# A hybrid decoder block on one core: the mixer's side work put in another order

## The chip, the core and the metric

The kernel runs on one core of a Trainium2 chip. The core has five engines with queues of their own: TensorE (PE, matmuls; the loads of its stationary operand are shown apart as PEld), VectorE (DVE), ScalarE (ACT), GpSimd (POOL) and SyncE (SP), and 16 DMA engines. Each engine works through its own list of instructions in order and waits on semaphores for the others. The metric is the time of one launch on the device, in microseconds (us).

## What is computed

One layer of a decoder block for 512 tokens of 1024 channels, in FP32. A modulation vector gives shift, scale and gate for the two halves. The first half, the mixer, projects the normalised tokens with one large matrix and feeds two branches: four retention heads, and four heads of a gated delta rule behind a short causal convolution. The second half is a mixture of 16 experts. Cut to what the change touches:

```python
mod = silu(c) @ mod_w + mod_b                       # 6 x 1024 columns
rq, rk, rv, rg, gq, gk, gv, gz, ga, gb, gate_a, gate_b = split_columns(xm @ w_in)
# retention, per head: (rope(q) k^T * decay) v, then RMS norm of each head's 256 columns
o_r = rms_norm(retention(rope(rq), rope(rk), rv));  y_ret = silu(rg) * o_r
# delta rule
qkv = silu(causal_conv(concat(gq, gk, gv), conv_w))  # 4 taps along the tokens
q, k = l2_normalize(...), l2_normalize(...)
beta = sigmoid(gb);  log_decay = -exp(a_log) * softplus(ga + dt_bias);  g_cum = cumsum(log_decay)
o_g = rms_norm(delta_rule(q, k, v, g_cum, beta)) * silu(gz)
h = x + gate * ((sigmoid(gate_a) * y_ret + sigmoid(gate_b) * o_g) @ w_out)
h = h + gate2 * moe(rms_norm(h) * (1 + scale2) + shift2)
```

## The kernel before

**The main projection.** Its columns are cut into blocks of 256: RQ0, RQ1, RK0, RK1 (T blocks), RV0 to RV3 (N blocks), the small block G with the eight columns ga and gb, then the T blocks GQ0, GQ1, GK0, GK1, GV0 to GV3, and the N blocks RG, GTA, GZ, GTB, four of each. A T block gives channels by tokens, an N block tokens by channels. Every FP32 operand is split into a rounded part hi (ScalarE, L293) and the rest lo (DVE, L294), and each product takes three passes. A block has two halves g (a T half has 24 matmuls, an N half 48, all at L1064), and `split_w(b + 1, ...)` splits the next block's weights meanwhile.

**The side work** stands in Python generators. Behind every piece of matmuls (8 in a T block, 16 in an N block, so three pieces in a half) the loop takes one step of `mods`, one of `convs` and one of `side`: what a generator issues up to its next `yield` goes into the engines' queues there. That alone sets the order on each engine; a step is no time, and a queue that comes late holds up whatever stands behind.

- `mods` (L488 to L520): the remaining 32 columns of the modulation. GpSimd fetches 512 KB (rawm, two buffers, L493), multiplies (L391) and adds 1024 to 128 in three operations (L393); PE sums over partitions with a matmul to one column (modp, L510) and DVE adds the bias (mcol, L511). The fetch of the next round is issued behind the column. While `state["subs"]` is set no round begins. Behind the last column PE transposes all of them (L516). At the first half of GZ0 the loop steps `mods` until it is done.
- `convs`: for each T half of GQ, GK and GV the convolution (ty: one ScalarE operation at L648, three of DVE at L650), the sigmoid (sg, L653), the product (gqT, gkT or vt, L656 and L678), then for GQ and GK the squares' sums on PE (L667) and for GV a transposition (vt, L684) and a scale (gv, L689).
- `side`: `gab_gen` turns ga and gb into beta and the cumulative decay (copy of g at L608; chain of small DVE operations L614 to L628; matmul gc at L632; transposition gct at L638). `ret_gen(h)`, one head after another, computes the scores (rs, L570), multiplies them by the decay into PT (L576, one buffer), sums outputs into PSUM (ro, L563) four steps later, takes squares' sums and copies the outputs over rv (ScalarE), and then norms them: a root on DVE, `rsqrt`, of 12 operations (L171 to L179), and two scales of rv (L586). Retention is done over the whole triangle of 512 tokens. Then `triangles` prepares the delta rule's triangular matrices (pre, L710; kk, L719) and solves them on GpSimd. The delta rule's chunks (`gdn_gen`) begin when that has been stored, with a transposition (tq, L762).

All PSUM tiles of the side work come from six banks in turn, `pst(...)`; a bank is taken again when the work on it six tiles ago is done. The main projection has two banks of its own.

## Time and profile before

| | us |
|---|---|
| median of three runs | 1087.81 |
| lowest and highest | 1086.55, 1091.23 |
| the profiled execution's own time | 1090.74 |
| its span in the trace | 1088.9 |
| PE busy in the span | 963.6 (88%) |
| DVE busy | 741.9 (68%) |
| ACT busy | 518.4 (48%) |
| POOL busy | 310.3 (28%) |

The stages by time in the trace: norm, modulation and first loads up to 61; RQ and RK to 90; RV to 138; G to 144; GQ, GK and GV to 302; RG from there, with GTA, GZ and GTB to about 577; output projection and routing to about 690; the experts to about 1040 and the tail. The trace names for each wait the instruction that ended it. The granted clock of PE is given as a share of its full speed: 1.0 is 2.4 GHz and 0.5 is 1.2 GHz.

### The profile page before, as it was taken

The page shows a single profiled execution, that of the slowest core. Times are in us where ns is not written, and L with a number is a line of the kernel's source. Part 1 is how long each engine was busy: PE and PEld are TensorE (multiplying, and loading weights), DVE is VectorE, ACT ScalarE, POOL GpSimd, SP SyncE. Part 2 cuts the span into 40 slices and gives each one's busy share as a digit, 9 for nine tenths or more (in the row PEclk, how much of TensorE's full clock was granted, in tenths as well). Part 3 has the DMA queues.
Part 4 walks back from the last instruction along what each step waited for, and adds up shares of the span by engine and source line. Part 5 has one row for each costly group of instructions (what it writes and reads, how often), then busy time and mean ns, then how long its engine had stood idle before and what let it go on. Part 6 is the DMA issues. An engine that isn't in the chain of part 4 may idle for free. (4 is left out here: it accounts for less than half of the span.)

```text
span 1088.9 us, 14847 instructions
## 1 busy us (share of the span) xinstructions
PE 963.6 (88%) x5672; PEld 834.7 (77%) x5672; DVE 741.9 (68%) x1163; ACT 518.4 (48%) x750; POOL 310.3 (28%) x285
## 2 busy tenths in 40 slices
PE   4899988989889999999989966699968899999973
PEld 2579957768788999999989965478756688888752
DVE  3478245767886673465458593699766889889777
ACT  4453134433342332263233433478645888878623
POOL 2018733553447555000010154111100211111144
PEclk8999998999989999999999988799989999999895
DMA  9857742232345532322157346789684999999931
GB/s 297 264 177 249 223 138 82 86 110 84 125 138 140 169 102 93 88 88 78 43 171 258 115 143 88 270 303 388 247 313 154 333 389 381 377 378 370 338 134 77
DMA packets 139538, 217.91 MB, mean 200 GB/s; under 512 B 14942, under 2 KB 72830, under 8 KB 138692
## 3 DMA queue, kind: packets, MB, share of 16 engines
q1 hardware_dynamic: 124640, 182.45, 49.3%
q0 software_dynamic: 11296, 30.66, 9.2%
q10 hardware_dynamic: 3524, 3.78, 1.0%
q8 instruction: 47, 0.77, 0.3%
q14 instruction: 31, 0.25, 0.1%
HBM read 204.98 MB, written 21.16 MB: 208 GB/s over the span
## 5 line engine op out<-in xcount | busy, mean ns | idle before, releaser
L294 DVE TENSOR_TENSOR lo<-raw,hi 128x1024 fp32r<-128x1024 f32 (+1 forms) x194 | 242.3, 1287 | 61.6 <-ACT hi L293 61.5
L293 ACT CAST hi<-raw 128x1024 fp32r<-128x1024 f32 (+1 forms) x198 | 197.5, 1043 | 34.6 <-PE gu L1492 27.3
L1064 PE MATMUL pm<-lo,xh 128*128 128x256 f32 x640 | 185.7, 290 | 12.2 <-DVE ty L650 7.0
L1064 PE MATMUL pm<-hi,xh 128*128 128x256 f32 x640 | 185.3, 290 | 0.0
L1064 PE MATMUL pm<-hi,xl 128*128 128x256 f32 x640 | 184.9, 289 | 0.0
L1064 PEld LDWEIGHTS pm<-lo,xh 128*128 128x128 f32 x640 | 124.9, 195 | 13.1 <-issue 7.2
L1064 PEld LDWEIGHTS pm<-hi,xh 128*128 128x128 f32 x640 | 124.9, 195 | 0.5
L1064 PEld LDWEIGHTS pm<-hi,xl 128*128 128x128 f32 x640 | 124.8, 195 | 0.3
L1492 PE MATMUL gu<-lo,xth 128*128 128x512 f32 x256 | 104.8, 409 | 10.3 <-DVE lo L1559 8.7
L1492 PE MATMUL gu<-hi,xtl 128*128 128x512 f32 x256 | 103.9, 406 | 2.0 <-DVE xtl L1460 2.0
L1492 PE MATMUL gu<-hi,xth 128*128 128x512 f32 x256 | 104.2, 407 | 0.0
L393 POOL TENSOR_TENSOR rawm<-rawm 128x512 f32<-128x512 f32 (+2 forms) x96 | 101.5, 1057 | 7.7
L493 POOL DMA_DIRECT2D rawm<-in_mod_w_dram x32 | 29.6, 925 | 210.7 <-PE modp L510 199.0
L1064 PE MATMUL pm<-xl,hi 128*128 128x512 f32 x168 | 70.1, 417 | 2.0 <-ACT hi L293 1.6
L1064 PE MATMUL pm<-xh,lo 128*128 128x512 f32 x168 | 71.3, 424 | 0.5 <-DVE lo L294 0.5
L1064 PE MATMUL pm<-xh,hi 128*128 128x512 f32 x168 | 70.9, 422 | 0.0
L1492 PEld LDWEIGHTS gu<-lo,xth 128*128 128x128 f32 x256 | 50.1, 196 | 23.3 <-DVE lo L1559 9.1
L1451 POOL DMA_INDIRECT X<-xfd,toks x14 | 20.2, 1446 | 151.8 <-PE xe L1472 131.4
L1008 ACT ACTIVATE sg<-pm 128x512 f32<-128x512 f32 x32 | 18.9, 597 | 91.1 <-PE pm L1064 77.1
L1514 PE MATMUL py<-lo,th 128*128 128x512 f32 x144 | 60.1, 417 | 1.3 <-ACT th L1505 1.3
L391 POOL TENSOR_TENSOR rawm<-rawm,cs 128x1024 f32<-128x1024 f32 x32 | 61.1, 1910 | 0.6
L1492 PEld LDWEIGHTS gu<-hi,xtl 128*128 128x128 f32 x256 | 50.0, 195 | 14.7 <-DVE xtl L1460 2.4
(405 smaller groups left out, 2056.4 us busy)
## 6 DMA issues: line engine op xcount, KB each, us to landing
raw<-in_w_in_dram SPq DMA_DIRECT2D x32, 1024.0 KB, 5.8
raw<-in_w_up_dram SPq DMA_DIRECT2D x26, 1024.0 KB, 13.6
raw<-in_w_gate_dram SPq DMA_DIRECT2D x24, 1024.0 KB, 11.0
raw<-in_w_down_dram SPq DMA_DIRECT2D x20, 1024.0 KB, 14.9
rawm<-in_mod_w_dram POOLq DMA_DIRECT2D x32, 512.0 KB, 5.2
rawe<-in_w_down_dram SPq DMA_DIRECT2D x9, 1024.0 KB, 16.0
rawe<-in_w_up_dram SPq DMA_DIRECT2D x8, 1024.0 KB, 16.9
mod<-in_mod_w_dram SPq DMA_DIRECT2D x7, 1024.0 KB, 12.5
```

What stands on the lines that cost most here:

```text
L293: act.copy(out=hi, in_=rw)
L294: (eng or dve).tensor_tensor(out=lo, in0=rw, in1=hi.bitcast(F32), op=ALU.subtract)
L391: pool.tensor_tensor(out=r, in0=r, in1=cs.unsqueeze(2).to_broadcast([P, KB, n]), op=ALU.mult)
L393: pool.tensor_tensor(out=r[:, :m], in0=r[:, :m], in1=r[:, m:2 * m], op=ALU.add)
L493: pool.dma_start(out=r, in_=mw[:, :, (16 + i) * P:(17 + i) * P])
L1008: act.activation(out=sg, in_=pt, func=AF.Sigmoid)
L1064: pe.matmul(o, lhsT=l, rhs=r, start=st, stop=sp__)
L1451: pool.indirect_dma_start(out=X, out_offset=None, in_=xfd, in_offset=bass.IndirectOffsetOnAxis(ap=at, axis=0), bounds_check=S - 1, oob_is_ ...
L1492: pe.matmul(pt, lhsT=xx[a][k // 4][:, k % 4], rhs=hi_lo[w][:, k % 4], start=(k == 0 and i == 0), stop=(k == KB - 1 and i == 2))
L1514: pe.matmul(pt, lhsT=tt[a][:, k], rhs=hi_lo[w][:, k], start=(k == 0 and i == 0), stop=(k == 3 and i == 2))
```

## The change

- **Retention** becomes one generator. It makes 16 score steps (four heads by four), issues an output's sums five steps behind its scores (`RL = 5`), uses a second PT buffer for the odd heads, copies a head out when its four outputs are issued, and takes one root for all four heads and then the eight scales, one head a step.
- **The modulation sums** go into two accumulators (acc) outside the fetched tile. A column is issued one round later, behind the sum of the next round. A round comes every three steps, in GQ, GK and GV every six. `subs` is set when the triangles begin, and not when their solution begins.
- **The gate block**: the weights of GQ0 are split ahead of the copy of g; the matmul gc is issued four side steps behind the chain and not one.
- **The triangles** issue the pre operations in steps of two, not four; the chunks of the delta rule wait four steps, not two, between the loads and the transposition tq.

```diff
-    def pool_sum(r, n):
+    def pool_sum(r, n, o):
...
-        for m in (4, 2, 1):
+        for m in (4, 2):
             pool.tensor_tensor(out=r[:, :m], in0=r[:, :m], in1=r[:, m:2 * m], op=ALU.add)
-        return r[:, 0]
+        pool.tensor_tensor(out=o, in0=r[:, 0], in1=r[:, 1], op=ALU.add)
...
+        accs = [tm.tile([P, P], F32, tag=f"acc{i}", name="acc", bufs=1) for i in range(2)]
+
+        def column(i):
+            pt = pst("modp")
+            pe.matmul(pt[:, :1], lhsT=accs[i % 2], rhs=ones[:, 0:1], start=True, stop=True)
+            dve.tensor_tensor(out=mcol[:, i:i + 1], in0=pt[:, :1], in1=cols[:, 16 + i:17 + i], op=ALU.add)
+
         nxt = fetch(0)
         for i in range(4 * KB):
             r = nxt
-            yield
+            for _ in range(6 if state.get("slow") else 3):
+                yield
             while state.get("subs"):
                 yield
             if i + 1 < 4 * KB:
                 nxt = fetch(i + 1)
             next(fills, None)
-            acc = pool_sum(r, P)
-            for _ in range(3 if i else NM):
-                yield
-            pt = pst("modp")
-            pe.matmul(pt[:, :1], lhsT=acc, rhs=ones[:, 0:1], start=True, stop=True)
-            dve.tensor_tensor(out=mcol[:, i:i + 1], in0=pt[:, :1], in1=cols[:, 16 + i:17 + i], op=ALU.add)
+            pool_sum(r, P, accs[i % 2])
+            if i:
+                column(i - 1)
+        for _ in range(4):
+            yield
+        column(4 * KB - 1)
...
+        n = NT * H
+        for s_ in range(n + RL + 1):
+            mul = scores(s_ // NT, s_ % NT) if s_ < n else None
+            o = s_ - RL
+            if 0 <= o < n:
+                out(o // NT, o % NT)
+            if o > 0 and o % NT == 0:
+                for i in range(2):
+                    evac(o // NT - 1, i)
+            yield
+            if mul:
+                mul()
+        for _ in range(2):
+            yield
+        rsqrt(st[:, 16:32], st[:, 0:16], 1.0 / DV, EPS)
+        for h in range(H):
+            yield
+            for i in range(2):
+                o = rv[i][:, :, h * DV:(h + 1) * DV]
+                dve.tensor_tensor(out=o, in0=o, in1=st[:, 16 + h * 4 + 2 * i:18 + h * 4 + 2 * i].unsqueeze(2)
+                                  .to_broadcast([P, 2, DV]), op=ALU.mult)
+            done["ret", h] = True
...
-        yield
+        for _ in range(4):
+            yield
         pt = pst("gc")
...
         sub = pool
+        state["subs"] = True
...
-            yield
+                if h % 2:
+                    yield
         act.activation(out=pre[:, NT:], in_=pre[:, NT:], func=AF.Exp, scale=-1.0)
...
-        yield
-        yield
+        for _ in range(4):
+            yield
         Q = u("Q")
...
+        state["slow"] = GQ <= c0 < GQ + 8 * 256
...
+            for hf in nxt:
+                split_w(b + 1, hf)
             side.add(gab_gen(pt))
             next(side.gens[-1])
-            for hf in nxt:
-                split_w(b + 1, hf)
```

**On DVE in the GK blocks.** The queue of DVE before, at the end of the first head's root (st) and up to the split of the next weights; PT is a block of masked scores, ty the convolution, rv the retention's values and outputs:

```order
L178 SCALAR_TENSOR_TENSOR na<-na,nx 128x4
L179 SCALAR_TENSOR_TENSOR st<-na,ny 128x4
L586 TENSOR_TENSOR rv_467<-rv_467,st 128x2x256
L586 TENSOR_TENSOR rv_468<-rv_468,st 128x2x256
L511 TENSOR_TENSOR mcol<-modp,cols 128x1
L576 TENSOR_TENSOR PT<-rs,decay 128x512
L576 TENSOR_TENSOR PT<-rs,decay 128x384
L650 SCALAR_TENSOR_TENSOR ty<-pm,cols,ty 128x511
L650 SCALAR_TENSOR_TENSOR ty<-pm,cols,ty 128x510
L650 SCALAR_TENSOR_TENSOR ty<-pm,cols,ty 128x509
L656 TENSOR_TENSOR gkT<-ty,sg 128x512
L294 TENSOR_TENSOR lo_93<-raw_88,hi_92 128x1024
```

And in the changed kernel, in the GK blocks too:

```order
L294 TENSOR_TENSOR lo_93<-raw_88,hi_92 128x1024
L502 TENSOR_TENSOR mcol<-modp,cols 128x1
L576 TENSOR_TENSOR PT<-rs,decay 128x512
L294 TENSOR_TENSOR lo_93<-raw_88,hi_92 128x1024
L576 TENSOR_TENSOR PT<-rs,decay 128x384
L576 TENSOR_TENSOR PT<-rs,decay 128x256
L677 SCALAR_TENSOR_TENSOR ty<-pm,cols,ty 128x511
L677 SCALAR_TENSOR_TENSOR ty<-pm,cols,ty 128x510
L677 SCALAR_TENSOR_TENSOR ty<-pm,cols,ty 128x509
L683 TENSOR_TENSOR gkT<-ty,sg 128x512
L576 TENSOR_TENSOR PT<-rs,decay 128x128
```

The root and the scales of rv are gone from here; all four PT operations of the third head stand here, where before the second head's began, among the convolutions and the lo of the splits.

**On DVE ahead of the last GV convolutions and RG0.** Before, the last head's scales and half of pre (the preparation of the triangles; gv are scaled values of the delta rule):

```order
L179 SCALAR_TENSOR_TENSOR st<-na,ny 128x4
L586 TENSOR_TENSOR rv_467<-rv_467,st 128x2x256
L586 TENSOR_TENSOR rv_468<-rv_468,st 128x2x256
L294 TENSOR_TENSOR lo_93<-raw_88,hi_92 128x1024
L710 SCALAR_TENSOR_TENSOR pre<-pre,gcum,sq 128x128 x4
L511 TENSOR_TENSOR mcol<-modp,cols 128x1
L710 SCALAR_TENSOR_TENSOR pre<-pre,gcum,sq 128x128 x4
L689 TENSOR_TENSOR gv_852<-vt,br 128x2x128
L689 TENSOR_TENSOR gv_853<-vt,br 128x2x128
L650 SCALAR_TENSOR_TENSOR ty<-pm,cols,ty 128x511
```

After, with the scales of two heads at the same place (rst holds all heads' roots):

```order
L294 TENSOR_TENSOR lo_91<-raw_89,hi_90 128x1024
L502 TENSOR_TENSOR mcol<-modp,cols 128x1
L612 TENSOR_TENSOR rv_467<-rv_467,rst 128x2x256
L612 TENSOR_TENSOR rv_468<-rv_468,rst 128x2x256
L294 TENSOR_TENSOR lo_91<-raw_89,hi_90 128x1024
L612 TENSOR_TENSOR rv_467<-rv_467,rst 128x2x256
L612 TENSOR_TENSOR rv_468<-rv_468,rst 128x2x256
L738 SCALAR_TENSOR_TENSOR pre<-pre,gcum,sq 128x128 x2
L716 TENSOR_TENSOR gv_854<-vt,br 128x2x128
L716 TENSOR_TENSOR gv_855<-vt,br 128x2x128
L677 SCALAR_TENSOR_TENSOR ty<-pm,cols,ty 128x511
```

The root of all heads begins 22 rows ahead of these, and the scales of the first two heads right behind it; the six other pre follow behind the convolution's product.

**On GpSimd in the first rounds of the modulation.** Before, a fetch behind the second sum, which waits for PE's column since it writes the tile that the column reads:

```order
L391 TENSOR_TENSOR rawm<-rawm,cs 128x1024
L393 TENSOR_TENSOR rawm<-rawm 128x512
L393 TENSOR_TENSOR rawm<-rawm 128x256
L393 TENSOR_TENSOR rawm<-rawm 128x128
L493 DMA rawm<-in_mod_w_dram 128x8x128
L391 TENSOR_TENSOR rawm<-rawm,cs 128x1024
```

After:

```order
L391 TENSOR_TENSOR rawm<-rawm,cs 128x1024
L393 TENSOR_TENSOR rawm<-rawm 128x512
L393 TENSOR_TENSOR rawm<-rawm 128x256
L394 TENSOR_TENSOR acc<-rawm 128x128
L493 DMA rawm<-in_mod_w_dram 128x8x128
L391 TENSOR_TENSOR rawm<-rawm,cs 128x1024
```

The last sum writes acc, and the fetch that follows needs only GpSimd's own sum; PE's columns are what a round waits for only from the third sum's acc onwards.

## Rows read from the trace of the kernel before

**Rows 1.** The page: busy time of the engines, then GB/s in 40 slices.

```profile
PE 963.6 (88%) x5672; PEld 834.7 (77%) x5672; DVE 741.9 (68%) x1163; ACT 518.4 (48%) x750; POOL 310.3 (28%) x285
...
GB/s 297 264 177 249 223 138 82 86 110 84 125 138 140 169 102 93 88 88 78 43 171 258 115 143 88 270 303 388 247 313 154 333 389 381 377 378 370 338 134 77
```

**Rows 2.** Waits of PE, 60 to 600: who waited for whom: total, times, longest us.

```profile
PE ro L563 <- DVE PT L576: 7.2, 3, 4.9
PE pm L1064 <- DVE ty L650: 7.0, 1, 7.0
PE pm L1064 <- ACT sg L1008: 5.1, 2, 2.9
PE gc L632 <- DVE glog L628: 4.0, 1, 4.0
PE modp L510 <- POOL rawm L393: 2.8, 2, 2.5
PE tq L762 <- DMA T<-dt: 2.0, 1, 2.0
PE pm L1064 <- ACT hi L293: 1.6, 1, 1.6
```

**Rows 3.** Windows: stretch, length, PE, PEld, DVE, ACT, POOL busy, granted clock, DMA share, GB/s.

```profile
145.49:253.70 108.21, 96.50 (x422) 77.84 (x423) 72.55 (x125) 40.23 (x69) 47.25 (x40) 0.91 0.34 105
253.70:302.23 48.53, 41.57 (x203) 34.30 (x201) 41.09 (x81) 17.35 (x36) 23.32 (x22) 0.95 0.42 130
147.66:151.07 3.41, 3.41 (x9) 2.08 (x8) 2.60 (x4) 0.62 (x1) 1.60 (x2) 0.50 0.55 163
164.72:174.96 10.24, 8.79 (x27) 7.44 (x28) 6.20 (x14) 5.93 (x8) 0.87 (x2) 0.50 0.00 0
239.82:246.65 6.83, 5.01 (x12) 3.97 (x13) 5.68 (x10) 0.96 (x2) 3.39 (x4) 0.50 0.60 192
297.84:308.08 10.24, 5.77 (x27) 5.80 (x28) 7.71 (x23) 4.25 (x4) 1.48 (x2) 0.50 0.33 103
352.45:355.86 3.41, 3.41 (x18) 3.41 (x18) 3.19 (x3) 0.00 (x0) 2.86 (x3) 0.50 0.94 225
362.69:366.10 3.41, 3.41 (x19) 3.41 (x18) 0.92 (x1) 1.68 (x2) 0.00 (x0) 0.50 0.05 17
```

**Rows 4.** Timeline of ACT at the gate block's end: start, duration, engine, line.

```profile
143.92 0.57 ACT L608 COPY g<-pm 8x512 f32<-8x512 f32 x1 [4.96 <-PE pm L1045]
```

**Rows 5.** Timelines of DVE and POOL in GQ0, the gate chain.

```profile
160.23 2.75 DVE L618 SCALAR_TENSOR_TENSOR tz<-tz 128x16 f32<-128x16 f32 x1
...
161.03 1.91 POOL L391 TENSOR_TENSOR rawm<-rawm,cs 128x1024 f32<-128x1024 f32 x1
```

**Rows 6.** Timelines of DVE and PE, first head's root, scales, PT, outputs.

```profile
203.40 1.25 DVE L171 TENSOR_SCALAR nx<-st 128x4 f32<-128x4 f32 x1
...
207.49 1.29 DVE L586 TENSOR_TENSOR rv<-rv,st 128x512 f32<-128x512 f32 x2
...
208.77 1.14 DVE L576 TENSOR_TENSOR PT<-rs,decay 128x512 f32<-128x512 f32 x2
...
209.50 0.70 PE L563 MATMUL ro<-rv,PT 128*128 128x256 f32 x2 [1.88 <-DVE PT L576]
```

**Rows 7.** Groups of instructions on PE, 145.4 to 302.2: count, busy, mean, idle.

```profile
L563 PE MATMUL ro<-rv,PT 128*128 128x256 f32 x80 | 21.5, 398 | 7.2 <-DVE PT L576 7.2
```

**Rows 8.** Timeline of DVE ahead of RG0: four pre, three convolution operations.

```profile
297.03 1.13 DVE L710 SCALAR_TENSOR_TENSOR pre<-pre,gcum,sq 128x128 f32<-128x128 f32 x4
...
299.87 2.30 DVE L650 SCALAR_TENSOR_TENSOR ty<-pm,cols,ty 128x511 f32<-128x511 f32 x3
```

**Rows 9.** Timeline of POOL: the second fetch's wait, a round's three adds.

```profile
77.31 0.93 POOL L493 DMA_DIRECT2D rawm<-in_mod_w_dram  x1 [56.26 <-PE modp L510]
...
95.60 4.71 POOL L393 TENSOR_TENSOR rawm<-rawm 128x512 f32<-128x512 f32 x3
```

**Rows 10.** Windows: RV, 90 to 138, columns as in rows 3.

```profile
90.00:138.00 48.00, 47.78 (x396) 47.30 (x395) 19.43 (x19) 11.28 (x17) 38.06 (x32) 1.00 0.74 225
```

More of the change, by code (lines that the diff above doesn't have):

```diff
@@ L551, in rope, with ret_gen, scores, out @@
         dve.tensor_tensor(out=rqk[:, h2], in0=rqk[:, h2], in1=sw, op=ALU.add)
-    def ret_gen(h):
-        PT = rp.tile([P, 1280], F32, tag="PT", name="PT", bufs=1)
+    def ret_gen():
+        RL = 5
         offs = [0, 512, 896, 1152]
-        po = []
-        def out(i):
+        PTs, pos_ = {}, {}
+        st = small.tile([P, 32], F32, name="rst")
+        def scores(h, jb):
+            if jb == 0:
+                PTs[h] = (slot(2, [P, 1280], F32, "PT") if h % 2 else
+                          rp.tile([P, 1280], F32, tag="PT", name="PT", bufs=1))
+            n = S - jb * P
+            pt = pst("rs")
+            pe.matmul(pt[:, :n], lhsT=rqk[:, H + h, jb * P:(jb + 1) * P], rhs=rqk[:, h, jb * P:],
+                      start=True, stop=True)
+            return lambda: dve.tensor_tensor(out=PTs[h][:, offs[jb]:offs[jb] + n], in0=pt[:, :n],
+                                             in1=decay[:, h, :n], op=ALU.mult)
+        def out(h, i):
@@ L559, in out @@
             if i % 2 == 0:
-                po.append(pst("ro"))
+                pos_.setdefault(h, []).append(pst("ro"))
             for jb in range(i + 1):
                 a = offs[jb] + (i - jb) * P
-                pe.matmul(po[-1][:, (i % 2) * DV:(i % 2 + 1) * DV], lhsT=PT[:, a:a + P],
+                pe.matmul(pos_[h][-1][:, (i % 2) * DV:(i % 2 + 1) * DV], lhsT=PTs[h][:, a:a + P],
                           rhs=rv[jb // 2][:, jb % 2, h * DV:(h + 1) * DV], start=(jb == 0), stop=(jb == i))
-        for jb in range(NT + 4):
-            if jb < NT:
-                n = S - jb * P
-                pt = pst("rs")
-                pe.matmul(pt[:, :n], lhsT=rqk[:, H + h, jb * P:(jb + 1) * P], rhs=rqk[:, h, jb * P:],
-                          start=True, stop=True)
-            if jb >= 4:
-                out(jb - 4)
-            yield
-            if jb < NT:
-                dve.tensor_tensor(out=PT[:, offs[jb]:offs[jb] + n], in0=pt[:, :n], in1=decay[:, h, :n], op=ALU.mult)
@@ L577, in ret_gen @@
-        st = tm.tile([P, 8], F32, tag="st", name="st", bufs=3)
-        for i in range(NT):
-            sumsq(po[i // 2][:, (i % 2) * DV:(i % 2 + 1) * DV], st[:, i:i + 1])
-        for i in range(2):
-            act.copy(out=rv[i][:, :, h * DV:(h + 1) * DV], in_=po[i].rearrange("p (t q) -> p t q", t=2))
-        yield
-        rsqrt(st[:, 4:8], st[:, 0:4], 1.0 / DV, EPS)
-        for i in range(2):
-            o = rv[i][:, :, h * DV:(h + 1) * DV]
-            dve.tensor_tensor(out=o, in0=o, in1=st[:, 4 + 2 * i:6 + 2 * i].unsqueeze(2).to_broadcast([P, 2, DV]),
-                              op=ALU.mult)
@@ L588, in ret_gen, with evac @@
-        done["ret", h] = True
+        def evac(h, i):
+            po = pos_[h][i]
+            for j in range(2):
+                sumsq(po[:, j * DV:(j + 1) * DV], st[:, h * 4 + i * 2 + j:h * 4 + i * 2 + j + 1])
+            act.copy(out=rv[i][:, :, h * DV:(h + 1) * DV], in_=po.rearrange("p (t q) -> p t q", t=2))
+        n = NT * H
[7 more added lines that the diff above has]
+                    evac(o // NT - 1, i)
+            yield
+            if mul:
+                mul()
@@ L733, in triangles @@
                 yield
-                state["subs"] = True
             to = [P, LB - 1 - c, c + 1]
@@ L756, in gdn_gen @@
         sp.dma_start(out=h4(pr), in_=gcd[ch * H:(ch + 1) * H].unsqueeze(0).to_broadcast([P, H, P]))
-        yield
-        yield
+        for _ in range(4):
+            yield
         Q = u("Q")
@@ L1131, in rets @@
             def rets():
-                for h in range(H):
-                    yield from ret_gen(h)
+                yield from ret_gen()
                 yield from triangles()
```

## The prediction

> **What bounds the kernel now.** I read the page first: TensorE (PE) is busy for 963.6 of 1088.9 us [rows 1]. It is the bound, so a change to the side work can only take back time in which PE stands still or runs at half clock. Next the waits of PE in the mixer, by the instruction that ended them, from 60 to 600 us [rows 2]. Six of the seven rows name work that the change touches: the retention's outputs wait 7.2 us for the masked scores PT on VectorE (DVE), the main projection 7.0 us for a convolution (ty) on DVE, the cumulative decay (gc) 4.0 us for glog, the modulation column (modp) 2.8 us for GpSimd's sum, the transposition tq 2.0 us for a DMA, and the first GQ block 1.6 us for a rounded weight (hi). The row of sg, 5.1 us, belongs to the end of the mixer and stays. Last, the granted clock by stretches [rows 3]: behind each of these waits stands a stretch at 0.5, the lower level (1.2 GHz). Half of PE's busy time in such a stretch is lost: 3.41 / 2 = 1.7 us at 147.66, 8.79 / 2 = 4.4 at 164.72, 5.01 / 2 = 2.5 at 239.82, 5.77 / 2 = 2.9 at 297.84, 1.7 at 352.45 and 1.7 at 362.69, so 14.9 in all. Every one begins at or behind a wait of at least 1.6 us. I take it that it goes with the wait. Behind the mixer PE is again the bound, and nothing there depends on when the mixer ends, so a gain in the mixer reaches the end.
>
> **The change part by part.** Terms are in us against the profiled execution's own 1090.74 (span 1088.9 and 1.8 around it), which lies 2.9 above the median of the runs, 1087.81.
>
> 1. *Splits of GQ0 ahead of the gate block's side work.* ScalarE's copy of g stood idle for 4.96 until 143.92, for the block's last matmul, and takes 0.57 [rows 4]; the rounding of the next block's weights stood behind it. Now it stands ahead, in that idle time. The wait of 1.6 and its half-clock stretch go; the 0.5 behind the second half's lo too. 1.6 + 0.5 + 1.7: **-3.8** (between -2.1 and -3.8).
>
> 2. *gc four side steps later.* The chain to glog ran on DVE from about 160 to 166. One of its 16-column operations took 2.75 there, beside GpSimd's multiplication that began at 161.03 and took 1.91 [rows 5]. PE waited 4.0 for the end and then lost 4.4. Four steps are 32 matmuls of the projection, at 96.50 / 422 = 0.23 [rows 3] some 7 us, which is more than the 4.0. I leave 1 for the places behind it (gct, and the l2 scales that use its result): -4.0 - 4.4 + 1 = **-7.4** (between -4 and -8.4).
>
> 3. *One root chain in place of four.* For each head 12 tiny DVE operations ran from 203.40 to 207.49 and two rv scales of 1.29 behind them; only then came the next head's PT, at 208.77, and PE waited 1.88 for it [rows 6]. In the new order PT has no root ahead of it. The 7.2 and the 2.5 of half clock go: **-9.7** (between -5 and -9.7).
>
> 4. *Retention is denser, and this is my largest unknown.* All four heads now end in GV0, two blocks earlier. About one head's outputs move into the stretch before 253.70: 21.5 / 4 = 5.4 of PE time [rows 7], **+5.4** there, and the same off the stretch behind it (in term 5). With side work this dense, PE is tied to DVE through six PSUM banks: a score's bank comes free only when its PT is through, and PT stands in DVE's queue behind a convolution (2.30 for three, [rows 8]) and one or two lo. I laid the DVE durations against PE's steps half-block by half-block over the ten half-blocks GQ0 to GV0, and got waits of about 9, most of them in GK1 and GV0; with 3 for clock, **+12**. Lower bound 0: DVE is busy 72.55 of 108.21 there [rows 3], loses two roots, and two steps of PE might cover its backlog. Upper bound 24: ten half-blocks at 1.9 (the wait before one PT) with half a us or so of clock each. I take the middle, since the new order has the backlog of convolution and lo but not that of the root.
>
> 5. *GV1 to RG0.* The root (once), the rv scales of all heads (eight operations) and eight more pre operations land here. Before, this took 48.53 us with DVE busy for 41.09 [rows 3], and a backlog that let PE wait 7.0. DVE's sum after: 41.1, less two roots (8.2) and a head's PT (about 2), plus one root (4.1), two more pairs of scales (2.6) and eight pre (2.3 by the row of four, 1.13 [rows 8]) = 39.9. Of DVE's 7.4 idle before I keep 3. That gives 43, bound by DVE: -5.5, and the half clock that reached past 302 gives half a us more, **-6** (0, if DVE's idle time stays as it is and the pre operations cost double, to -9).
>
> 6. *GpSimd.* Sums now go to two accumulators and PE reads a column one round later; the rounds pause while GpSimd solves the triangles. The wait of 2.5 near 352 and its 1.7, and the wait of tq for its DMA near 362 (the loads now stand two yields further ahead of it) with its 1.7, go: **-7.9** (between -4 and -7.9). Three columns are left for a drain at GZ0, where PE meets them back to back: **+2.5**, from 0 (sums ready) to 6 (one round, below).
>
> 7. *The start.* GpSimd stood idle for 56.26 up to 77.31, since its next fetch waited for PE's column [rows 9]. Without that wait two more fetches of 0.5 MB fall into the first 50 us, where the DMA moves 297 and 264 GB/s in the first two slices [rows 1], twice the 105 and 130 of the mixer's middle [rows 3], and the first loads are what all else waits for: 1 MB / 0.3 MB per us = **+3** (0 to 6, the upper end if GpSimd's two sums also hold up DVE).
>
> 8. *The longer drain of chunks 2 and 3 at GTB*, bound by PE: **+0.5** (0 to 2).
>
> Sum: -3.8 - 7.4 - 9.7 + 5.4 + 12 - 6 - 7.9 + 2.5 + 3 + 0.5 = -11.4, so 1079.3 in a profile and 1087.8 - 11.4 = **1076.4** as a median.
>
> The row of 2.75 for 16 columns shows DVE standing still until GpSimd's multiplication ends. The Trainium skill ("SBUF — State Buffer", Who interferes with whom) says that a DVE instruction with two SBUF inputs and a GpSimd instruction that reads SBUF exclude one another for a whole instruction, and the trace agrees: the operation ends at 162.98, the multiplication at 162.94. By that rule the twelve rounds between 145 and 302 that become seven free DVE of some five multiplications, at most 10 us, which would make the sum about -15; by the rows, which show PE waiting for DVE at a few places only, it is nothing that I can count, and I leave it out.
>
> **The rivals.** *The clean case:* the backlog of term 4 is covered, no wait comes and the clock stays up. Then -11.4 - 12 = -23.4, 1064.4, or 1066 with a us or two left over. For it: DVE has a third of its time free before 253.70. Against it: that is a mean, and the waits in [rows 2] come from bursts. *Coupling:* term 4 at its upper end, 24 in place of 12: 1088.4, nothing gained. For it: one root alone made PE wait 1.88, a convolution and two lo are as long, and the clock falls behind waits of 1.6 already. *The change does not reach its place:* its two safest edits (terms 1 and 2, -11.2) depend on nothing else, so this would be about what coupling gives, and shares its chance. *The slow case, GpSimd bound in RV:* from 90 to 138 GpSimd was busy for 38.06 with 32 instructions, five to a round: 5.9 a round [rows 10]. The new order has eight columns there in place of six, one per three side steps, about 6 us. At 5.9 and with one round of lead this just holds. But a round beside much DVE work took 0.93 + 1.91 + 4.71 = 7.5 [rows 5, 9]; eight of these are 60 in 48, less a lead of about one round, 7.5: PE waits some 4.5 in RV, and each wait may cost a half-clock stretch of 1.7 to 4.4. With four of these at 3 that is 16.5, and the rounds that are late come back at the drain (6 in place of 2.5): -11.4 + 16.5 + 3.5 = +8.6, **1096**. It decides from 17 us of new waits in RV and at the drain upwards; a wait of PE for acc in RV of more than a us would be its mark. Against it: the mean of 5.9, in which such long rounds are already counted.
>
> **How the numbers follow.** My forecast, the middle of term 4: 0.47. Clean: 0.18. Coupling: 0.23. GpSimd bound: 0.12. The forecast and the clean case are both faster by over 0.5% (below 1082.4), which is about what a measurement of this kernel can tell from no change; the coupling is within it, the last slower (above 1093.2). So 0.65, 0.23, 0.12. The range leaves out the slow case and the lower half of the clean one: 1066 to 1092, where the upper end is coupling with the start at its 6.
>
> **What the profile after would show.** Right: no wait of gc for glog nor of ro for PT above a us, a first GQ block without gap, clock 1.0 from 145 to 175; GV0's convolution done about 5 earlier and RG0 about 11 earlier. PE's new waits, for banks (rs, ro or pm waiting for PT, ty, or ScalarE's copy), between 150 and 240, about 9 in sum. In GV1 to GV3 DVE almost without idle time. In the first 60 us GpSimd with three sums, and PE's start about 3 later. Wrong: waits for banks above 20, rows at 0.5 that last as long as before, or acc among PE's waits in RV.

## The result: one per cent slower, and the profile after

The changed kernel takes 1098.14 us (median of six runs, 1095.98 to 1100.88); the kernel before, in six runs, 1086.32 (1085.64 to 1091.23). The ratio is 1.0097 with an interval of 1.007 to 1.0124: slower by about 11 us, where the prediction had faster by 11. The profiled execution took 1095.98 with a span of 1094.2. Its page, busy time of the engines, against [rows 1]:

```profile
PE 961.1 (88%) x5672; PEld 833.4 (76%) x5672; DVE 732.5 (67%) x1127; ACT 518.4 (47%) x750; POOL 315.9 (29%) x285
```

PE is no busier than before and DVE has 9 less: the loss is time in which PE stands still.

Who waited for whom on PE from 60 to 600 us in the changed kernel (total, times, longest us); it answers to [rows 2]:

```profile
PE pm L1093 <- DVE ty L677: 15.6, 4, 9.1
PE pm L1093 <- ACT sg L1036: 5.4, 2, 2.9
PE ro L584 <- DVE mcol L502: 4.2, 1, 4.2
PE modp L501 <- POOL acc L394: 4.1, 3, 3.0
PE rs L574 <- DVE mcol L502: 2.4, 1, 2.4
PE pm L1093 <- DVE sg L1038: 2.3, 1, 2.3
```

The waits for glog (gc), hi, the first PT and tq have gone. In their place stand 15.6 for convolutions (7.0 before), 6.6 for banks behind mcol, and 4.1 for GpSimd's sum (2.8 before).

The two profiled executions shown first lie badly for a comparison: that of before is near the top of its runs, that of after is the lowest of its own, and their spans differ by 5.3 only. Both kernels were therefore profiled once more. These spans differ by 11.8, as the medians do, so the account below goes by this pair, though each was taken on another chip. The windows of both, cut at the copy of g, where ScalarE takes up the first convolution of GV0 and that of GV2, at the end of RG0's first half, and at the end of GTB (stretch, length, PE busy; then PEld, DVE, ACT, POOL, granted clock, DMA share, GB/s). Before, profiled again:

```profile
0.00:144.46 144.46, 123.16 (x811) 101.78 (x811) 68.53 (x97) 53.71 (x81) 57.97 (x56) 0.95 0.72 229
144.46:231.39 86.93, 78.82 (x360) 63.51 (x361) 56.52 (x82) 39.61 (x68) 41.01 (x35) 0.96 0.37 113
231.39:271.34 39.95, 35.05 (x157) 28.70 (x156) 31.66 (x77) 11.61 (x23) 17.20 (x15) 0.91 0.30 92
271.34:312.09 40.75, 33.70 (x189) 30.18 (x188) 32.98 (x64) 15.86 (x26) 17.61 (x18) 0.87 0.36 117
312.09:576.55 264.46, 254.50 (x2018) 248.31 (x2017) 155.90 (x305) 85.48 (x156) 75.03 (x86) 0.99 0.39 116
576.55:1087.19 510.64, 435.07 (x2143) 359.91 (x2142) 396.46 (x542) 311.80 (x400) 100.25 (x76) 0.92 0.76 266
```

The changed kernel, profiled again:

```profile
0.00:149.12 149.12, 125.43 (x816) 103.59 (x817) 73.43 (x101) 55.52 (x84) 76.71 (x72) 0.92 0.75 236
149.12:238.82 89.70, 82.65 (x374) 66.67 (x373) 49.18 (x73) 40.81 (x76) 35.41 (x29) 0.96 0.32 97
238.82:277.39 38.57, 34.11 (x158) 28.17 (x157) 24.06 (x57) 11.39 (x22) 1.55 (x4) 0.96 0.18 55
277.39:317.99 40.60, 29.90 (x174) 26.25 (x173) 26.66 (x54) 13.21 (x16) 0.00 (x0) 0.83 0.26 85
317.99:588.00 270.01, 257.44 (x2016) 250.94 (x2015) 162.20 (x304) 85.33 (x156) 100.83 (x106) 0.97 0.41 122
588.00:1098.98 510.98, 437.15 (x2142) 361.30 (x2141) 396.29 (x541) 312.28 (x400) 101.55 (x76) 0.92 0.75 265
```

Length less PE busy is idle time. The fourth row is the one to look at: in the changed kernel DVE has only 26.7 us of work in 40.6 and GpSimd none, and still PE stands still for 10.7. For GV1 to RG0, which ends within this row, term 5 had forecast 6 less. The account, by the lengths:

| stretch | terms | forecast | measured |
|---|---|---|---|
| start to the copy of g | 7 | +3 | +4.7 |
| copy of g to the end of RG0's first half | 1 to 5 | -9.5 | +1.2 |
| from there to the end of GTB | 6, 8 | -4.9 | +5.6 |
| behind | none | 0 | +0.3 |
| sum | | -11.4 | +11.8 |

### The profile page after: what moved, and what is told of

The parts are those of the page before. It is cut to its first block, busy times and chain, and to the rows that moved or that the text cites. A ratio compares the mean times of both kernels' runs of the same rounds, so it can differ in the third digit from the quotient of the medians.

```text
span 1094.2 us, 14841 instructions
## 1 busy us (share of the span) xinstructions
PE 961.1 (88%) x5672; PEld 833.4 (76%) x5672; DVE 732.5 (67%) x1127; ACT 518.4 (47%) x750; POOL 315.9 (29%) x285
## 3 DMA queue, kind: packets, MB, share of 16 engines
q1 hardware_dynamic: 124640, 182.45, 48.6%
## 5 line engine op out<-in xcount | busy, mean ns | idle before, releaser
L294 DVE TENSOR_TENSOR lo<-raw,hi 128x1024 fp32r<-128x1024 f32 (+1 forms) x194 | 252.6, 1340 | 58.3 <-ACT hi L293 58.2
L393 POOL TENSOR_TENSOR rawm<-rawm 128x512 f32<-128x512 f32 x64 | 84.1, 1314 | 5.2
L1093 PE MATMUL pm<-xl,hi 128*128 128x512 f32 x168 | 69.6, 415 | 16.0 <-DVE ty L677 15.6
L1036 ACT ACTIVATE sg<-pm 128x512 f32<-128x512 f32 x32 | 19.0, 596 | 96.8 <-PE pm L1093 85.1
L294 DVE TENSOR_TENSOR lo<-rawe,hi 128x1024 fp32r<-128x1024 f32 x48 | 56.3, 1220 | 5.5 <-ACT hi L293 5.5
```

The source lines that it names most:

```text
L294: (eng or dve).tensor_tensor(out=lo, in0=rw, in1=hi.bitcast(F32), op=ALU.subtract)
L393: pool.tensor_tensor(out=r[:, :m], in0=r[:, :m], in1=r[:, m:2 * m], op=ALU.add)
L1036: act.activation(out=sg, in_=pt, func=AF.Sigmoid)
L1093: pe.matmul(o, lhsT=l, rhs=r, start=st, stop=sp__)
```

## Reading the three losses

**Ahead of RG0: one late load.** SP, DVE and PE in the changed kernel's first profile (start, duration, engine, line, and in brackets the idle time before with what ended it):

```profile
277.65 0.37 SPq L285 DMA_DIRECT2D raw<-in_w_in_dram  x1
278.14 0.50 SPq L728 DMA_DIRECT2D pre<-gcd  x1
```

```profile
276.40 1.22 DVE L294 TENSOR_TENSOR lo<-raw,hi 128x1024 fp32r<-128x1024 f32 x1
277.54 1.28 DVE L612 TENSOR_TENSOR rv<-rv,rst 128x512 f32<-128x512 f32 x2
285.42 0.61 DVE L738 SCALAR_TENSOR_TENSOR pre<-pre,gcum,sq 128x128 f32<-128x128 f32 x2 [6.60 <-DMA pre<-gcd]
285.96 0.75 DVE L716 TENSOR_TENSOR gv<-vt,br 128x256 f32<-128x256 f32 x2
286.62 2.31 DVE L677 SCALAR_TENSOR_TENSOR ty<-pm,cols,ty 128x511 f32<-128x511 f32 x3
```

```profile
289.08 0.76 PE L1093 MATMUL pm<-xl,hi 128*128 128x512 f32 x1 [9.14 <-DVE ty L677]
```

SP's load of pre stands behind the load of the next raw weights, which waits until lo has read the old ones (277.62). The load of pre goes out at 278.14 and DVE's first pre can start at 285.42, 7.3 later. Behind it on DVE stand gv and the convolution, and for that PE waits 9.14. The clock falls with it, as the window shows (columns as above):

```profile
282.13:292.37 10.24, 3.29 (x8) 2.65 (x9) 6.12 (x16) 1.21 (x2) 0.00 (x0) 0.50 0.25 101
```

Before, the same load was followed by the last head's root, scales and a lo, and DVE had no wait for it. SP and DVE of before, profiled again:

```profile
274.00 1.53 SPq L701 DMA_DIRECT2D pre<-gcd  x1
```

```profile
294.74 1.14 DVE L710 SCALAR_TENSOR_TENSOR pre<-pre,gcum,sq 128x128 f32<-128x128 f32 x4
```

20.7 us lay between load and first use. The work that the change removed from this place was what hid the load.

**The start.** GpSimd in the changed kernel now fetches at 21.77 and 29.20 too, where before it stood still until 77.31 [rows 9]:

```profile
21.77 0.93 POOL L493 DMA_DIRECT2D rawm<-in_mod_w_dram  x1 [0.30 <-POOL acc L394]
...
29.20 0.92 POOL L493 DMA_DIRECT2D rawm<-in_mod_w_dram  x1 [0.30 <-POOL acc L394]
```

PE's first modulation matmul (L416, duration, then first and last start), before and then after:

```profile
L416 PE MATMUL pm<-xl,hi x7: 389/507/629, 32.8 to 44.7; 128*128 128x512 f32 x7
```

```profile
L416 PE MATMUL pm<-xl,hi x4: 389/597/767, 36.7 to 40.3; 128*128 128x512 f32 x4
```

It starts 3.9 later, as SP's next load of raw does (33.81 before, 37.73 after), and the copy of g comes 4.1 later in this pair and 4.7 in the second. All twenty profiles agree on the first step: this matmul starts at 36.1 to 36.7 in the seven whose program lets the two early fetches out, `p_mods` among them, and at 31.7 to 33.0 in the other thirteen.

**The banks in GK.** DVE in the changed kernel, around the first wait for a bank of 4.21 on PE:

```profile
204.57 1.48 DVE L294 TENSOR_TENSOR lo<-raw,hi 128x1024 fp32r<-128x1024 f32 x1 [1.69 <-ACT hi L293]
205.97 0.15 DVE L502 TENSOR_TENSOR mcol<-modp,cols 128x1 f32<-128x1 f32 x1
206.04 0.67 DVE L576 TENSOR_TENSOR PT<-rs,decay 128x512 f32<-128x512 f32 x1
```

```profile
206.17 0.70 PE L584 MATMUL ro<-rv,PT 128*128 128x256 f32 x2 [4.21 <-DVE mcol L502]
```

mcol, which frees the bank, takes 0.15, but stands behind a lo, which waits 1.69 for ScalarE's hi.

## Experiments: two suspects

The load and the two early fetches were taken away, each alone and both together, beside the unchanged kernel.

> The changed kernel once more, beside the kernel before on this chip, for a second trace of it. All theories: 8 to 13 us slower than before. The wait of the pre operations for their DMA near 279 (6.6 us on VectorE, 9.1 us of TensorE behind it) and the later start (4.6 us) are there again if they belong to the kernel and not to one execution.

Measured: 1099.18, ratio 1.0108 (1.0065 to 1.0151).

`e1_hoist` issues the load of pre behind the last scores:

```diff
             if mul:
                 mul()
+            if s_ == n - 1:
+                state["pre"] = rp.tile([P, 2 * H, S], F32, tag="rqk", name="pre")
+                sp.dma_start(out=state["pre"][:, 0:NT]..., in_=gcd...)
```

> The changed kernel, with the 1 MB load of pre issued behind the last scores of the retention (in GV0) and not when the triangles begin (end of GV2). Nothing else moves. Theory A (the change put pre's first operations right behind their load on VectorE, so that a convolution stood behind a DMA): the wait of 6.6 us and the 9.1 us of TensorE go, with some 2 to 3 us of half clock behind them: 9 to 12 us faster than the changed kernel, about equal to before. Theory B (coupling of TensorE and VectorE through the PSUM banks is the loss): under 3 us faster, since another wait of the same kind takes its place.

Measured: 1095.28, 1.0041 (1.0008 to 1.0075). The load goes out at 245.65, DVE has no wait for it, and the waits of PE for ty from 262 to 300 are 7.2, the longest 3.8. From the convolution of GV2 to that of GV3's second half it takes 25.7 in place of 32.7 in the changed kernel profiled beside it: 6.9 back, as the row said. The median moved only 4, less than theory A's 9 and more than theory B's 3. The profiled execution, which lies at the median, gives the rest away ahead of this place: from the copy of g to the end of GV0's second convolution it takes 112.7 in place of 107.0, 2.7 of that in the gate chain by a collision of DVE and GpSimd (last section), and it has 6.8 at half clock at 192.5 and at 212.9 each, where the changed kernel has 3.4 twice. Two of the ten runs took 1085.3 and 1086.7, 14 and 12 below the changed kernel; whether the collision is absent in them no trace shows.

`e2_gate` leaves the first sum in rawm, so that the third fetch waits for PE's column again:

```diff
...
-            pool_sum(r, P, accs[i % 2])
+            o = accs[i % 2] if i else r[:, 0]
+            pool_sum(r, P, o)
             if i:
-                column(i - 1)
+                column(i - 1, last)
+            last = o
...
```

> The changed kernel, but the first sum stays in its fetched tile and its column reads it there, so that the third fetch waits for TensorE's first column again, as before. Theory A (two more fetches of 0.5 MB in the saturated first 60 us put the first projection off): 4 to 5 us faster than the changed kernel, the first full matmul of the projection at 61 and not 66. Theory B (the first 60 us only vary from run to run): no difference, within 1 us.

Measured: 1106.95, 1.0169 (1.0145 to 1.0194), 8 slower than the changed kernel, which neither theory had: the cause is right and the cure loses. The first main matmul starts at 59.6 in place of 66.8, so the two early fetches are what delays it. But the lead they gave is gone, and one round per three steps is too much for GpSimd: from 60 to 160 PE now has

```profile
PE modp L501 <- POOL acc L394: 4.9, 4, 2.4
```

and at the copy of g (149.5) the 7 us are lost again. This is the prediction's slow rival, in a kernel that takes the lead away. The further loss lies up to GV0's second convolution, 112.9 in place of 107.0: here too an operation of the gate chain takes 2.45 beside GpSimd, as in `e1_hoist`.

`e3_both`, both edits:

> Both edits together, the earlier load of pre and the third fetch held back. Theory A: the gains add, 13 to 17 us faster than the changed kernel and 2 to 6 us faster than before. Theory B (coupling): under 8 us faster than the changed kernel, so no faster than before.

Measured: 1102.58, 1.0115 (1.008 to 1.0149), 3 slower than the changed kernel and outside both theories. The hoist takes 4.4 off `e2_gate`, as it took 3.9 off the changed kernel; the collision is in this trace as well (2.50).

## Experiments: the parts alone

The kernel before, with one part of the change each. `p_gab` has the splits ahead of the copy of g and gc after four steps, `p_ret` the one generator of retention, `p_mods` accumulators, rates and pause.

```diff
-        yield
+        for _ in range(4):
+            yield
         pt = pst("gc")
```

```diff
-                for h in range(H):
-                    yield from ret_gen(h)
+                yield from ret_gen()
```

```diff
+            for _ in range(6 if state.get("slow") else 3):
+                yield
...
+            pool_sum(r, P, accs[i % 2])
```

> The kernel before once more, for a second trace of it, since its first profiled execution lay 4.4 us above the median of its runs. Theory P (the place of GpSimd's multiplications against VectorE's small operations differs from execution to execution): the stretch of the gate chain, or the root before RG0, takes 2 to 6 us less in this trace than in the first. Theory Q (the runs differ in the clock of the experts' part): the mixer ends at the same time, the rest differs.

> The kernel before with the gate block's part of the change alone: the next block's weights split ahead of the copy of g, and the matmul gc four side steps later. Theory A (the waits of 1.6, 0.5 and 4.0 us and the half clock behind them go, nothing else is touched): 6 to 10 us faster than before. Theory B (what is taken back here is given back to the next wait, for PT): under 3 us.

> The kernel before with the retention's part of the change alone: one pipeline, a second PT buffer, one root. Theory A (the root of the last head and its scales, some 8 us of VectorE, used to cover the load of pre; without them pre waits for it): TensorE's waits for PT (7.2 us) go, but a wait of VectorE for pre's load of 4 us or more appears near 280 and TensorE's wait for ty stays at 7 or more; in sum within 4 us of before. Theory B (coupling through the banks alone): no wait for the load, and waits for banks of over 10 us in GQ to GV; slower than before by 4 or more.

> The kernel before with the modulation's part of the change alone: two accumulators, columns a round later, rounds every three or six steps, paused from the triangles' beginning. Theory A: the start is 4 to 5 us later, two or three us come back where fewer rounds fall into GQ to GV, and the wait near 350 stays: 1 to 6 us slower than before. Theory B (fewer rounds beside VectorE's chain in GQ to GV are worth more): 3 us faster or more.

Measured, against the kernel before on the same chip (1090.19): `p_gab` 1087.2, 0.9961 (0.994 to 0.9982), some 4 us; `p_ret` 1097.37, 1.0051 (1.0019 to 1.0083), 6 slower; `p_mods` 1087.9, 0.9976 (0.995 to 1.0003), 2 or 3 faster, though its interval reaches no change. The profiled execution of before took 1088.97. The parts do not add up to +11. The pre operations in steps of two and the longer lag of tq were not run alone in the kernel before; `f4_nolag` below clears the lag. With that left open, what hurts arises where the parts meet. In `p_gab` the gate block's waits go, but the waits for PT behind the retention's roots, 6.8 in the second profile of before, have grown:

```profile
PE ro L563 <- DVE PT L576: 12.5, 4, 7.4
```

In `p_ret` the load of pre is early enough; there the loss is another one. Its waits for ty are 21.6, since the root, eight scales and the pre operations meet GpSimd's rounds, which are not paused here. Two rows of DVE from that place:

```profile
283.43 1.13 DVE L728 SCALAR_TENSOR_TENSOR pre<-pre,gcum,sq 128x128 f32<-128x128 f32 x4
285.62 6.49 DVE L728 SCALAR_TENSOR_TENSOR pre<-pre,gcum,sq 128x128 f32<-128x128 f32 x8
```

Four operations take 1.13 and the next eight 6.49; beside the eight GpSimd fetches at 285.90, multiplies from 286.84 and adds up to 291.43.

## Experiments: order in the queues

`e5_order` issues, in GQ to GV, the steps of mods, convs and side ahead of the split of the next weights, so that mcol, PT and SP's load of pre stand ahead of hi, lo and raw:

```diff
-                    if nxt:
+                    if nxt and not state["slow"]:
                         split_w(b + 1, nxt.pop(0))
...
                     side.step()
+                if (n + 1) % piece == 0 and nxt and state["slow"]:
+                    split_w(b + 1, nxt.pop(0))
```

> The changed kernel, but in GQ, GK and GV each step of the modulation, the convolutions and the retention is issued ahead of the split of the next weights, not behind it, so that mcol and PT no longer stand behind lo on VectorE. Theory A (TensorE's waits for banks held by mcol, 2.4 and 4.2 us, and the half clock behind them come from that place in the queue): these waits go, 6 to 10 us faster than the changed kernel. Theory B (VectorE is the bound there, whatever the order): the waits only change their names, within 3 us of the changed kernel.

Measured: 1086.5, 0.9972 (0.9947 to 0.9998): the one edit takes off 12 by the medians (that of the changed kernel is from another chip), 14 by the ratios. Of the two waits that theory A names, rs's 2.4 is gone and ro's is still 3.7. From its windows, with the same cuts (second and fourth of the six):

```profile
149.14:234.20 85.06, 81.39 (x374) 66.13 (x373) 51.08 (x74) 40.74 (x76) 34.78 (x29) 0.96 0.33 103
...
272.96:305.96 33.00, 32.20 (x194) 28.39 (x193) 26.16 (x52) 13.11 (x16) 0.00 (x0) 0.94 0.23 72
```

85.1 in place of 89.7, and 33.0 in place of 40.6 with 0.8 idle. The load of pre now goes out 18 us ahead of its use:

```profile
258.80 0.52 SPq L728 DMA_DIRECT2D pre<-gcd  x1
```

`f3_order_early` does the same up to GV0 only, so that the banks gain and the load stays late:

```diff
-                    if nxt:
+                    if nxt and not (GQ <= c0 < GV + 256):
                         split_w(b + 1, nxt.pop(0))
...
+                if (n + 1) % piece == 0 and nxt and GQ <= c0 < GV + 256:
+                    split_w(b + 1, nxt.pop(0))
```

> The changed kernel with the steps ahead of the splits in GQ, GK and GV0 only; from GV1 on as in the changed kernel, so that the load of pre again stands behind a weight load on SyncE. Theory A (two causes: banks in GK, some 6 us, and the load of pre, some 7 to 10): 4 to 8 us faster than the changed kernel, and the wait of pre for its load of 6 us or more is there. Theory B (the banks are all of it): as fast as e5_order, 11 to 13 us faster than the changed kernel.

Measured: 1094.79, 1.0067 (1.0036 to 1.0098). The load goes out at 275.58, and the wait is there in full:

```profile
PE pm L1093 <- DVE ty L677: 12.4, 2, 10.9
```

So of the 12 to 14, some 8 by the medians and 10 by the ratios belong to the load and the order in GV1 to GV3, and 3 to 4 to the order in GQ to GV0.

`e4_late` lets the third fetch wait for the last normalised channels, by a one-column copy on GpSimd:

```diff
+            if i == 1:
+                pool.tensor_copy(out=gate1, in_=xT[:, KB - 1, 0:1])
             if i + 1 < 4 * KB:
                 nxt = fetch(i + 1)
```

> The changed kernel, but GpSimd's third fetch of a modulation tile waits for the last normalised and modulated channels (about 55 us) by reading one column of them. Unlike the gate on TensorE's first column this keeps the lead of one round for RV. Theory A (the extra 1 MB in the saturated start costs 4.7 us): the copy of g comes at 144 to 146 and not 148 to 149, no new waits for acc in RV, 3 to 5 us faster than the changed kernel. Theory B (GpSimd needs that early lead): waits for acc of 3 us or more in RV, no gain.

Measured: 1104.89, 1.0139 (1.0101 to 1.0178). The first main matmul comes at 59.9, but the two rounds then run at 61 and 67 beside DVE's splits; RQ and RK take 8 longer, and the start is lost again (copy of g at 150.3). From there to GV0's second convolution it takes 111.3, again with the collision (2.64).

`e6_all` (hoist, late fetch and order) and `g1` (the kernel before with the gate block's and the modulation's part and the late fetch):

> Three edits on the changed kernel: the load of pre behind the last scores, the third fetch held to about 55 us, the steps ahead of the splits. Theory A: the losses add, 15 to 22 us faster than the changed kernel, 4 to 10 faster than before. Theory B (something else eats it, as GpSimd's multiplications against VectorE): not faster than before.

> The kernel before with two parts of the change, the gate block's and the modulation's, and with the third fetch held to about 55 us; retention and lags as before. Theory A (these parts add up, 3 and 2 us, and the held fetch gives the start back, 4): 6 to 10 us faster than before. Theory B (they take the same waits): 2 to 4 us faster than before, no more than the gate block's part alone.

Measured: 1089.06, 0.9997 (0.9974 to 1.002), no better than the order alone; and 1085.21, 0.9948 (0.993 to 0.9967): with retention left as it was, this makes the kernel faster.

## Experiments: mending, lags, and a version that beats both

`f1_mended` is the order with the gate of `e2_gate` and slower rounds ahead of G (four steps, five in GQ to GV); `f5` has four steps in both. `f4_nolag` is the changed kernel with the lag of tq at two steps.

```diff
-            for _ in range(6 if state.get("slow") else 3):
+            for _ in range(5 if state.get("slow") else 4 if i < 10 else 3 if i < 99 else 3):
```

> The changed kernel with the steps ahead of the splits in GQ to GV (as e5_order), the third fetch held back by TensorE's first column (as e2_gate), and rounds of GpSimd every four steps before G and every five in GQ to GV, in place of three and six. Theory A (the start's loss is the two early fetches, and RV needs the lead only at three steps a round): the first full matmul of the projection at 60 to 62, no waits for acc before G, 4 to 6 us faster than e5_order, so 1081 to 1083. Theory B (the columns that are put off come back as waits in RG to GZ): 1086 or more.

> As f1_mended, but GpSimd's rounds come every four steps in GQ to GV too, so that three columns and not four are left for the drain at GZ0. Theory A (f1_mended lost its gain to a last round of GpSimd that the drain had to wait for): the waits for acc fall from 15.7 to under 8 us, the mixer ends 10 us or more earlier than in f1_mended, 1078 to 1084. Theory B (each round in GQ to GV costs as much beside VectorE's work as it saves at the drain): 1088 or more.

> The changed kernel with two steps, not four, between the loads of a chunk of the delta rule and its transposition tq. Theory A (the longer lag costs what RG to GTB lost): 3 to 6 us faster than the changed kernel. Theory B (the lag is neutral: work moves from GTA and GZ into the drain at GTB, and TensorE is the bound in both): within 2 us, with a wait of tq for its load of 2 us back.

Measured: `f1_mended` 1098.24, 1.0067 (1.0029 to 1.0105). It saves the start (copy of g at 142.9) without waits for acc in RV, but the columns it puts off come back behind the pause, from 300 to 470:

```profile
PE modp L501 <- POOL acc L394: 15.7, 5, 5.7
```

`f5` 1086.69, 0.9979 (0.9955 to 1.0004): here the copy of g comes at 141.9 and the waits for acc are 3.9 in all, but the mixer takes 431.0 where `e5_order` took 422.5: rounds every four steps in GQ to GV sit beside more of DVE's work (4.8 of wait for a bank and 10.1 for ty, 3.7 and 7.0 in `e5_order`). The start's gain is paid there. `f4_nolag` 1099.77, 1.0086 (1.0056 to 1.0116), no different from the changed kernel: GTB is 5 shorter and GTA 8 to 10 longer, so the longer drain at GTB is work that moved.

`f2_gab_order` is the kernel before with the gate block's part and the order, `g2` has the new retention as well:

> The kernel before with the gate block's part, and the steps ahead of the splits in GQ to GV; retention, modulation and lags as before. Theory A (PT and mcol stand behind lo in the kernel before too): the waits for PT shrink from 12.5 to under 8 us, 7 to 12 us faster than before. Theory B (the roots, not the lo, are what PT waits for): no faster than the gate block's part alone, 3 to 5 us faster than before.

> The kernel before with the gate block's and the retention's part, and the steps ahead of the splits in GQ to GV; modulation and lags as before, so that nothing of the start is touched. Theory A (the retention pipeline gains once its PT and mcol no longer stand behind lo): 3 us or more faster than f2_gab_order (1082), so 1079 or less. Theory B (with GpSimd's rounds as before, the root, the scales and pre are too much for VectorE in GV1 to RG0): slower than f2_gab_order by 3 us or more.

Measured: `f2_gab_order` 1082.02, 0.9924 (0.9896 to 0.9952), the fastest of all: 8 below the kernel before on the same chip and 16 below the changed kernel's median. It lies 4 below `p_gab`, by ratios whose intervals just overlap. Its profiled execution took 1086.24, the highest of its four runs, so the trace places the 8 us poorly; it shows no wait for glog or hi any more and the old wait for PT still there (8.5, where theory A had under 8). `g2` 1091.16, 1.0015 (0.9989 to 1.0042): ahead of RG0 the new retention loses what the order gives, by waits for ty of 17.3 in five places, with GpSimd's rounds not paused.

## Why the prediction was wrong

**The step that failed: term 5, GV1 to RG0.** I summed DVE's work to 39.9, left it 3 of idle time and took the stretch as bound by it. DVE had time to spare (26.7 of work in the last 40.6), but its first pre waited 6.6 for a load whose cover, the last head's root and scales, the change removes. The prediction costs the root at a gain only, names neither this load nor what hid it, and none of its rows is one of SP. By its own cuts, from the end of GV0's second convolution on DVE to RG0's first matmul, the stretch took 48.6 in both profiles of before and 50.7 and 52.1 in those of the changed kernel: -6 was forecast, +2.1 and +3.5 came. The changed kernel, profiled again, and `e1_hoist` (columns as above):

```profile
256.14:308.23 52.09, 36.93 (x164) 29.96 (x162) 36.78 (x76) 16.39 (x28) 0.00 (x0) 0.84 0.25 81
```

```profile
262.37:306.41 44.04, 36.87 (x163) 29.99 (x162) 35.62 (x73) 15.18 (x28) 0.00 (x0) 0.88 0.23 72
```

The changed kernel and its variants divide by the load alone. The six profiles with the late load (the changed kernel twice, `e2_gate`, `e4_late`, `f3_order_early`, `f4_nolag`) have DVE wait 6.6 to 7.0 for it and take 50.7 to 52.1; the six with an early one (`e1_hoist`, `e3_both`, `e5_order`, `e6_all`, `f1_mended`, `f5`) have no such wait and take 42.8 to 45.2. So the load is the cause, worth 7 to 8 here by the hoist alone (52.1 to 44.0, and 52.0 in `e2_gate` to 45.2 in `e3_both`).

That the stretch then takes the 43 of the forecast is in part luck, for it is not bound as the sum had it: DVE works 35.6 of these 44.0, not 39.9 of 43. The sum did not count that GpSimd now pauses there (23.4 of work before, 0 after). `p_mods`, with the pause and the old retention, takes 44.6 with 35.4 of DVE, where before has 41.1; `p_ret` and `g2`, with the new retention and no pause, take 60.5 and 57.8 without any wait for the load. No run shows a gain of the new retention itself in this stretch.

**Term 6, GpSimd: right price, wrong place.** The wait of tq went, that for the sums did not: 6.7 in the second profile. GpSimd of the changed kernel behind the pause, first profile:

```profile
344.53 1.91 POOL L391 TENSOR_TENSOR rawm<-rawm,cs 128x1024 f32<-128x1024 f32 x1
346.53 3.29 POOL L393 TENSOR_TENSOR rawm<-rawm 128x512 f32<-128x512 f32 x2
349.90 1.32 POOL L394 TENSOR_TENSOR acc<-rawm 128x128 f32<-128x128 f32 x1
351.51 0.93 POOL L493 DMA_DIRECT2D rawm<-in_mod_w_dram  x1 [0.30 <-POOL acc L394]
```

Fetch to fetch that is 7.9 with the fetch of 0.93 ahead; three N steps, half a block, are 5.9. I had worked out 7.5 for a round beside DVE, and put it against RV only, where a lead covers it. From the end of RG0's first half to the end of GTB -4.9 was forecast and +5.6 came: 2.6 more of idle time, 3.4 more by half clock (four stretches of 3.41 in place of two, half of each lost), and 0.4 less work. Why the clock fell twice more there was not isolated. In `e5_order` this part still takes 265.7, 1.2 above the kernel before, so its gain isn't recovered there either.

**Term 4, the banks: near in size, elsewhere in place.** From the copy of g to the end of GV0's second convolution, terms 1 to 4 say -3.5; both kernels, profiled again, take 107.0. The waits that I expected from banks, about 9, were 6.6, at mcol behind lo rather than at PT. That the sum of the terms lies near does not show each of them: see the next ones. What I had not seen is that part of these waits goes without touching retention: `e5_order` and `f3_order_early` take 102.4 and 101.8 here, by whether the split or the side step is issued first.

**Terms 1 to 3.** The waits of hi, lo, gc and the first PT went. But the 4.4 of half clock behind gc was a matter of that execution: in the second profile of before the stretch is 3.41 long, 1.7. And taken alone the gate block's part brought 4, not 11, beside longer waits for PT (`p_gab`).

**Term 7, the start: +3 forecast, +4.7 measured**, by the mechanism named, and within its bounds. **Term 8** (+0.5) is moved work: GTB takes 83.4 in place of 77.6 with 39 more matmuls of PE (620 for 581), and RG, GTA and GZ together have 39 fewer. The rivals: coupling did not come; GpSimd as the bound in RV came only in `e2_gate` and `e3_both`, which have no lead.

What stays open: the expected -11 against the kernel before was not reached by any version that keeps the new retention. `e5_order` ends 3 to 4 below it and `f5` 2 below it, which its interval does not tell from no change, `f5` with a start 7 earlier than `e5_order` and a mixer 8 longer; rounds that are slow enough for DVE and early enough for PE were not found.

## What to carry to other kernels

Before counting removed work as a gain, list the transfers issued ahead of it and used behind it: their landing time becomes the next wait (here 6.6 us, and 9.1 on the engine that is the bound). Where two streams share an in-order queue, issue first what frees a resource and takes 0.2 us, then what takes 1.2 and waits for others; this swap brought 3 to 4 us in GQ to GV0, and 8 to 10 more in GV1 to GV3, where it also put the load of pre ahead, more than any part of the rewrite. Price a periodic task (a round of 7.5) against every stretch in which it is due, above all behind a pause, and judge a part of a change with the others in place: three parts were -4, +6 and -3 (the last within noise) alone, and the whole +11.

## What the runs showed of the hardware

A shift of less than 0.1 us between GpSimd and DVE can cost 2.6 on DVE. The last operation of the gate chain in the changed kernel (profiled again), with GpSimd beside it:

```profile
166.03 0.17 DVE L654 SCALAR_TENSOR_TENSOR glog<-tz,alb 128x16 f32<-128x16 f32 x1
```

```profile
165.99 0.93 POOL L493 DMA_DIRECT2D rawm<-in_mod_w_dram  x1 [0.62 <-POOL acc L394]
166.94 1.91 POOL L391 TENSOR_TENSOR rawm<-rawm,cs 128x1024 f32<-128x1024 f32 x1
```

and in `e1_hoist`, with the same code there, DVE and GpSimd:

```profile
166.69 2.79 DVE L658 SCALAR_TENSOR_TENSOR glog<-tz,alb 128x16 f32<-128x16 f32 x1
```

```profile
166.57 0.93 POOL L493 DMA_DIRECT2D rawm<-in_mod_w_dram  x1 [0.62 <-POOL acc L394]
167.52 1.91 POOL L391 TENSOR_TENSOR rawm<-rawm,cs 128x1024 f32<-128x1024 f32 x1
```

One operation starts 0.04 behind the fetch and takes 0.17, the other 0.12 behind it and takes 2.79, until GpSimd's multiplication is through (169.43); it begins 0.8 ahead of that multiplication. Other traces agree: in the changed kernel's first profile glog begins 0.06 behind the fetch (164.98 and 164.92) and takes 0.17; in the kernel before the operation of 2.75 [rows 5] begins 0.14 behind the fetch at 160.09 and ends with the multiplication. Runs of one program may differ by such places, as `e1_hoist` ran between 1085.3 and 1099.7, but only one of its runs was traced, so this is not shown. The Trainium skill ("SBUF — State Buffer", Who interferes with whom) has the two engines share a pair of ports under an exclusive lock. The end of the long operation agrees with that (169.48 against 169.43); that it is held already during the fetch no run here explains.
